# The last block of a hybrid encoder: pools divided by when their rows are done, operand buffers opened earlier, raw weights on another queue

## The chip, the cores and the metric

The kernel runs on one core of a Trainium2 chip. The metric is the device time of one execution in microseconds; of several runs the median is taken. The engines are PE (TensorE, matmuls; PEld is its weight load), DVE (VectorE), ACT (ScalarE), POOL (GpSimd) and SP (SyncE). Each has its own instruction stream and executes it in order. Here SP and POOL also issue the DMAs, each in the order of its own stream; "SPq" and "POOLq" in the profile are these DMA-issuing rows.

## The reference

One layer (DEPTH is 1) over 2048 prompt frames, 16 meta frames and 64 sample frames, all in f32, with D_MODEL = 1024 and D_FF = 2816:

```python
def _swiglu(h, wg, wu, wd):
    return (jax.nn.silu(h @ wg) * (h @ wu)) @ wd
...
        m, ns = _mixer(_rmsnorm(x, p['norm1_w'][l]), l, *st, segs, p)
        x = x + m
        x = x + _swiglu(_rmsnorm(x, p['norm2_w'][l]), p['w_gate'][l], p['w_up'][l], p['w_down'][l])
...
    return _rmsnorm(x, p['final_norm_w']), [jnp.stack(lst) for lst in new]
```

`_mixer` projects its input, runs three groups of recurrent heads (SSD, RWKV-7, HGRN2) and ends with the output projection `y @ w_out`. The change touches only that output projection and the SwiGLU of the last 1024 frames.

## The kernel before, in words

The prompt is cut into 17 tiles of 128 frames. Nine of them (EARLY, three blocks of three) get their output projection and their feed-forward part by the class of `fs`, beside the recurrent heads of later tiles; the last early block's feed-forward part (`fs[-1].ffn` from SWITCH on, then `fs[-1].rest()`) runs after all heads are done. The last eight tiles (LATE: two halves h of NH = 4 tiles) come then as one block, and everything below is about that block.

Every f32 product is made of three matmuls of values split in a high and a low part: ACT casts the high part (`S.activation`), DVE subtracts it for the low part. `to_parts` does that for operands, at L1416 (ACT) and L1417 (DVE), and `parts` for weights, at L1355 and L1356. All matmuls are issued by one helper, L111.

The block's matrices are taken in quarters: tokens by half, input columns by half, output columns by half. Instead of eight quarter products there are seven, listed in PRODS with operands a (a11, s3, s2, a22, s1, a12, s4: quarters of the left matrix or their sums and differences) and b (b11, t3, t2, t4, t1, b21, b22: quarters of the weights or their sums and differences t1 to t4). The b quarters were split before and lie in DRAM as pairs; SP loads them (L216, "w<-w", 512 KB). The t quarters are sums: those of "wo" and of the first PRE = 3 column pairs were prepared in DRAM, SP loads them (L1364) and `parts` splits them. For the later column pairs the four raw quarters are loaded (L1538, "lraw", 256 KB each), summed on DVE (L1540 to L1543) and split. All split weights go through a ring of WB = 5 buffers "w", raw ones through RB = 3 buffers "raw".

The steps of the block are:

1. "wo", by `tokens_first`: seven products into PSUM banks (g by `xbank`, d by `ybank`, four each), added on DVE to the rows `acc[h][j]`. Its operands are made by `y_group` from the mixers' outputs ya, in pairs, in tiles of `op_tile` ("op", four buffers in the pool lq). The sums s1, s2, s3, s4 of ya are made at L1458 to L1464.
2. `second_half` (beside the last products of "wo") and `first_half`: rows of the second and the first half are normalised (`scaled`, w2k at L246), transposed on PE (`turned`, L1480), and made into the operands `hop` of the columns; differences at L1511, L1512 and L1519.
3. `columns`, the gate and up projections by pairs of columns: class Pair steps a generator for gate and one for up side by side. Each of the seven steps is one product of 12 matmuls for gate and one for up. Results are copied out of PSUM by ACT (c11, c12, c21, c22 at L1558) or added on DVE (L1561); `finish` (L1610 to L1616) makes silu(gate) * up and its sums, and POOL stores them ("ma", "ms", L1619).
4. "wd", by `tokens_first` again, with operands loaded by SP in `m_group` (L1645); then the final norm. The t sums of w_down are made beside the columns: POOL loads the raw quarters (L1319, "raw<-in_w_down"), DVE sums them (L1327 to L1335), POOL stores them (L1324).

The order in each engine's stream is set by a scheduler that simulates the program; a tile of a pool that is opened on the place of an earlier one waits until the earlier one's users are done. Such pools are what the change moves: before, lq opens after `stE.close()` (the early block's pools), and lp (which holds c and lraw) opens on the place of the pool lo, whose rows first_half still uses.

Of the kernel before, what the change touches and what calls it, by code (L numbers as in the profile page):

```python
# [19 lines left out]
P = 128  # L20
# [58 lines left out]
def body(tc, A, O, blocks=None, supers=None, dbg=None):  # L79
# [7 lines left out]
    def pool(st, name, bufs=1, **kw):  # L87
        return st.enter_context(tc.tile_pool(name=name, bufs=bufs, **kw))
# [1195 lines left out]
    if supers:  # L1284
# [86 lines left out]
        def tokens_first(key, order, per, group, acc, then, ahead, behind):  # L1371
# [3 lines left out]
            for a, b, x, fresh, (h, d) in PRODS:  # L1375
# [32 lines left out]
                        behind(j)  # L1408
                then(a)

        def op_tile(tag="op"):
            o = mk(lq, [P, 2, 4, 512], F32, tag=tag, bufs=4) if tag == "op" else mk(lqa, [P, 2, 4, 512], F32, tag=tag, bufs=3)
            return o[:, 0].bitcast(F32R), o[:, 1].bitcast(F32R)

        def to_parts(hi, lo, src):
# [14 lines left out]
        for m in (2, 0, 1):  # L1430
            ya[m] = mk(lqa, [P, 2, 4, 512], F32, tag="ya", bufs=3)
            for h in range(2):
                for j in range(NH):
                    nc.sync.dma_start(ya[m][:, h, :, j * P:j * P + P], yscr[m][tile_of(h, j)])
        flow(fs[-1].ffn(SWITCH, NFF))
        flow(fs[-1].rest())
        stE.close()
        lq = pool(st, "lq", side="right", reuse_waits="tile")


        stO = ExitStack()
        lo_ = pool(stO, "lo", reuse_waits="tile")
        acc = [[mk(lo_, [P, D], tag=f"acc{h}{j}", bufs=1) for j in range(NH)] for h in (1, 0)][::-1]
        for h in (0, 1):
            for j in range(NH):
                G.dma_start(acc[h][j], x_rows(tile_of(h, j))[0][0])
# [58 lines left out]
        def first_half(j):  # L1505
# [10 lines left out]
            if j + 2 < NH:  # L1516
# [4 lines left out]

        tokens_first("wo", [4, 5, 0, 1, 2, 3], 2, y_group, acc, second_rows, second_half,
                     lambda j: scaled(0, j) if j < 2 else None)
        for n, tag in (("a11", "ya"), ("s3", "ya"), ("s2", "op"), ("a12", "op"), ("s4", "op")):
            hop[n] = op_tile(tag)


        msc = {(n, g): dram.tile([P, 4, 512], F32, tag=f"m{n}{g}", name=f"m{n}{g}") for n, *_ in PRODS for g in range(3)}
        stF = ExitStack()

        def columns(key, i):

            q = dict(zip(("b11", "b12", "b21", "b22"), quarters(key, i)))
            raw = {}
            if i >= PRE:
                for n in ("b22", "b12", "b11", "b21"):
                    raw[n] = mk(lp, [P, 512], tag="lraw", bufs=8)
                    nc.sync.dma_start(raw[n], q[n])  # L1538
                b11, b12, b21, b22 = (raw[n] for n in q)
                V.tensor_tensor(b22, b22, b12, SUB)  # L1540
                V.tensor_tensor(b12, b12, b11, SUB)
                V.tensor_tensor(b11, b22, b11, ADD)
                V.tensor_tensor(b21, b21, b11, SUB)  # L1543
                raw = {"t3": b22, "t1": b12, "t2": b11, "t4": b21}

            def prod(ps, a, b, first=True):
                hi, lo = parts(raw[b]) if b in raw else b_part(key, i, b)
                ah, al = hop[a]
                for k in range(4):
                    wh, wl = (x[:, k * P:(k + 1) * P] for x in (hi, lo))  # L1550
                    mm(ps, wh, ah[:, k], first and k == 0, False, not first)
                    mm(ps, wh, al[:, k], False, False, not first)
                    mm(ps, wl, ah[:, k], False, k == 3, not first)

            def copy(tag, ps, bufs):
                r = mk(lp, [P, 512], tag=tag, bufs=bufs)
                with tc.high_priority() if i < PRE else ExitStack():
                    S.activation(r, ps, AF.Copy)  # L1558
                return r

            add = lambda r, ps: V.tensor_tensor(r, ps, r, ADD)  # L1561
            pre = i < PRE
            x = xbank()
            prod(x, "s1", "t1")
            c22 = copy("c22", x, 6)
            yield
            y = xbank() if pre else ybank()
            prod(y, "a22", "t4")
            c21 = copy("c21", y, 6)
            yield  # L1570
            z = ybank()
            prod(z, "a11", "b11")
            c11 = copy("c11", z, 4)
            yield
            y = ybank()
            prod(y, "a12", "b21")
            add(c11, y)
            yield
            prod(z, "s2", "t2", False)
            c12 = copy("c12", z, 4)  # L1580
            yield
            if pre:
                add(c12, c22)
                x = xbank()
            prod(x, "s4", "b22", pre)
            add(c12, x)
            yield
            prod(z, "s3", "t3", False)
            add(c21, z)
            add(c22, z)  # L1590
            return c11, c12, c21, c22
# [28 lines left out]

        for j in range(NH):
            first_half(j)
        stO.close()
        lm = pool(st, "lm", side="right", reuse_waits="tile")
        lp = pool(stF, "lp", reuse_waits="tile")
        pairs = [Pair(i) for i in range(PRE)]
        for p_ in pairs:
            p_.step()
            p_.step()
        for i in range(NFF // 2):  # L1630
            if i >= PRE:
                pairs.append(Pair(i))
# [147 lines left out]
```

## Time and profile before

| what | value |
|---|---|
| median of 3 runs | 3547.19 us (3545.42 to 3551.86) |
| the profiled execution | 3539.1 us |
| its span | 3537.3 us |
| mean granted clock of PE | 0.982 |
| PE busy | 3367.3 us (95%) |
| POOL busy | 745.9 us (21%) |
| DMA moved | 860 MB, 243 GB/s over the span |

A row of a timeline has the start, the duration, the engine, the line of the kernel, the operation, the tiles out<-in, how many in a row, and in brackets the idle time before it and who ended it. A row of waits has the engine and the tile that waited, the one waited for, the total in us, how often, and the longest. A row of windows has, for each engine, busy time and count of instructions, and at the end the granted clock, the DMA share and GB/s. The last block runs from about 2726 us to the end.

### The profile page before, as it was taken

To read this page: it belongs to the slowest core of one execution; us is meant where nothing else is said; L and a number is where in the kernel's file an instruction comes from. 1 tells how busy PE (TensorE), PEld (TensorE's weight loads), DVE (VectorE), ACT (ScalarE), POOL (GpSimd) and SP (SyncE) were. 2 spreads that over 40 slices of the span, in tenths; PEclk is the share of its full clock that TensorE was granted. 3 is DMA by queue.
4 is the path that set the end of the run, shared out by engine and by line. 5 is a ranking of instruction groups with operands and counts; after the bars stand their busy time and mean duration, and the time that the engine had idled before them with its cause. 6 is when DMAs were issued, how large, how long until landed. Compare 5 with 4: busy or idle time off the path is not lost.

```text
span 3537.3 us, 61018 instructions
## 1 busy us (share of the span) xinstructions
PE 3367.3 (95%) x22588; PEld 2940.6 (83%) x22588; DVE 2216.0 (63%) x4961; ACT 1227.5 (35%) x2635; POOL 745.9 (21%) x1058
## 2 busy tenths in 40 slices
PE   7999999999999998889898999999989989999999
PEld 7999789899799996778786899879988868778887
DVE  3358556568666677687876767666524666555553
ACT  4445333244333444344342222222111352223342
POOL 3324202102112112444442120110101003320101
PEclk9999999999999998999999999999999999999999
DMA  9776875565775668888889898686688548775866
GB/s 323 232 229 212 296 228 166 162 174 171 247 225 172 193 198 266 290 308 302 298 312 329 308 325 269 208 286 220 222 278 261 185 141 284 272 264 170 289 202 214
DMA packets 431218, 860.41 MB, mean 243 GB/s; under 512 B 112432, under 2 KB 212280, under 8 KB 428872
## 3 DMA queue, kind: packets, MB, share of 16 engines
q1 hardware_dynamic: 403592, 765.79, 66.1%
q0 software_dynamic: 27328, 90.72, 6.9%
q8 instruction: 178, 2.92, 0.3%
q14 instruction: 120, 0.98, 0.1%
HBM read 603.81 MB, written 252.54 MB: 242 GB/s over the span
## 4 chain that ended last, share of the span: by engine, by line
PE 64%; DMA 13%; DVE 11%; issue 6%; POOL 2%; ACT 2%; SPq 2%; POOLq 0%; DVEq 0%; ACTq 0%
PE g L111 46%; PE d L111 8%; PE c L111 4%; PE h L111 3%; DMA w<-w 3%; DMA raw<-in_w_down 2%; DVE tp L640 1%; DVE Xp L641 1%; DMA hin<-hg 1%; DMA raw<-in_w_up 1%; POOL w L222 1%; DMA hg<-stage 1%; DVE gcv L418 1%; DMA dec<-cu 1%; DVE acc L1278 0%
## 5 line engine op out<-in xcount | busy, mean ns | idle before, releaser
L111 PE MATMUL g<-hhi,w 128*128 128x384 f32 (+3 forms) x3312 | 832.0, 330 | 10.3 <-DMA w<-w 4.1
L111 PEld LDWEIGHTS g<-hhi,w 128*128 128x128 f32 (+1 forms) x3312 | 579.9, 188 | 24.3 <-POOL w L222 4.3
L111 PE MATMUL g<-h2hi,w 128*128 128x384 f32 (+1 forms) x2112 | 549.5, 336 | 19.5 <-DMA w<-w 6.7
L111 PE MATMUL g<-hlo,w 128*128 128x384 f32 (+3 forms) x1680 | 551.2, 328 | 0.0
L111 PEld LDWEIGHTS g<-h2hi,w 128*128 128x128 f32 x2112 | 376.6, 190 | 33.4 <-ACT w L220 7.7
L111 PE MATMUL g<-h2lo,w 128*128 128x384 f32 (+1 forms) x1056 | 349.9, 332 | 0.0
L111 PEld LDWEIGHTS g<-hlo,w 128*128 128x128 f32 (+1 forms) x1680 | 313.9, 187 | 6.8 <-issue 0.9
L222 POOL TENSOR_TENSOR w<-raw,w 128x512 fp32r<-128x512 f32 x180 | 246.7, 1373 | 343.8 <-ACT w L220 273.0
L111 PE MATMUL g<-w,mhi 128*128 128x512 f32 x792 | 259.2, 403 | 12.0 <-DMA w<-w 4.0
L220 ACT ACTIVATE w<-raw 128x512 fp32r<-128x512 f32 x240 | 150.3, 629 | 207.9 <-PE g L111 58.3
L111 PEld LDWEIGHTS g<-h2lo,w 128*128 128x128 f32 x1056 | 200.4, 190 | 2.9
L111 PE MATMUL g<-w,op 128*128 128x512 f32 x816 | 194.4, 397 | 3.1 <-ACT op L1416 3.1
L111 PEld LDWEIGHTS g<-w,op 128*128 128x128 f32 x816 | 153.4, 189 | 41.6 <-ACT op L1416 3.5
L111 PEld LDWEIGHTS g<-w,mhi 128*128 128x128 f32 x792 | 144.5, 188 | 48.3 <-DVE acc L1278 7.6
L111 PE MATMUL g<-w,hhi 128*128 128x512 f32 (+1 forms) x544 | 176.3, 404 | 7.4 <-DMA w<-w 4.3
L111 PE MATMUL d<-op,w 128*128 128x512 f32 x720 | 168.8, 392 | 2.8 <-DVE w L1356 2.8
L111 PEld LDWEIGHTS d<-op,w 128*128 128x128 f32 x720 | 135.0, 188 | 33.5 <-DVE w L1356 4.1
L1278 DVE TENSOR_TENSOR acc<-g,acc 128x512 f32<-128x512 f32 (+1 forms) x198 | 132.1, 682 | 44.0 <-PE g L111 43.9
L640 DVE TENSOR_TENSOR tp<-Xp,b4k 128x60 f32<-128x60 f32 (+24 forms) x527 | 126.8, 241 | 51.2 <-DMA b4k<-psc 38.3
L111 PE MATMUL g<-w,mlo 128*128 128x512 f32 x396 | 155.6, 393 | 0.0
L111 PE MATMUL d<-w,op 128*128 128x512 f32 x612 | 143.9, 395 | 0.0
L111 PEld LDWEIGHTS d<-w,op 128*128 128x128 f32 x612 | 114.7, 187 | 28.1
(437 smaller groups left out, 6233.0 us busy)
## 6 DMA issues: line engine op xcount, KB each, us to landing
w<-w SPq DMA_DIRECT2D x893, 512.0 KB, 4.4
hin<-hg SPq DMA_DIRECT2D x16, 1280.0 KB, 8.4
rin<-rw SPq DMA_DIRECT2D x16, 896.0 KB, 7.1
raw<-in_w_gate SPq DMA_DIRECT2D x56, 256.0 KB, 4.5
raw<-in_w_up SPq DMA_DIRECT2D x56, 256.0 KB, 4.5
hg<-stage SPq DMA_DIRECT2D x64, 192.0 KB, 2.5
raw<-in_w_out SPq DMA_DIRECT2D x48, 256.0 KB, 4.6
sin<-ss SPq DMA_DIRECT2D x16, 768.0 KB, 4.9
```

Of the source, the lines that this page charges most:

```text
L111: return T.matmul(out, lhsT, rhs, start=start, stop=stop, skip_group_check=more)
L220: S.activation(hi, raw, AF.Copy)
L222: (G if units[0] % 4 < GLO else V).tensor_tensor(lo, raw, wt[:, 0], SUB)
L418: V.scalar_tensor_tensor(cvt[:, :M], raw[:, j:j + M], tap(j), cvt[:, :M], MUL, ADD)
L640: V.tensor_tensor(tv, _bc(Xp[:, 0:m, q], 2, w), _bc(Up[:, q, q + 1:32], 1, m), MUL)
L641: V.tensor_tensor(Xp[:, 0:m, q + 1:32], Xp[:, 0:m, q + 1:32], tv, ADD)
L1278: V.tensor_tensor(self.acc[:n, i, cs], ps[:n], self.acc[:n, i, cs], ADD)
```

## The change

There are three parts.

- Operand tiles: three buffers "op" in lq, which is opened before the early block's last part (`fs[-1].ffn`); every fourth operand tile instead lies in "opx", one buffer in a pool lqx, opened where lq was.
- Pools by when their rows are done: the second half's rows acc[1] lie in a pool of their own (lo1), closed right after "wo". On that place a new pool lc holds c21 and c22 (c22 with four buffers instead of six). The pool of the other rows is closed, and lm and lp are opened, only after the early steps of the first three pairs. For these pairs the first step is now a22·t4 (c21) and the second s1·t1 (c22), and the last of them does only its first step ahead, so that ten products instead of twelve stand before the first a11·b11.
- lraw: ten buffers instead of eight, loaded from POOL's stream instead of SP's (64 loads).

```diff
         def op_tile(tag="op"):
-            o = mk(lq, [P, 2, 4, 512], F32, tag=tag, bufs=4) if tag == "op" else mk(lqa, [P, 2, 4, 512], F32, tag=tag, bufs=3)
+            if tag == "op":
+                opn[0] += 1
+                p, tag, bufs = (lq, "op", 3) if opn[0] % 4 else (lqx, "opx", 1)
+            else:
+                p, bufs = lqa, 3
+            o = mk(p, [P, 2, 4, 512], F32, tag=tag, bufs=bufs)
...
+        lq = pool(st, "lq", side="right", reuse_waits="tile")
         flow(fs[-1].ffn(SWITCH, NFF))
         flow(fs[-1].rest())
         stE.close()
-        lq = pool(st, "lq", side="right", reuse_waits="tile")
-        stO = ExitStack()
+        lqx = pool(st, "lqx", side="right", reuse_waits="tile")
+        stO, stO1, stF = ExitStack(), ExitStack(), ExitStack()
         lo_ = pool(stO, "lo", reuse_waits="tile")
-        acc = [[mk(lo_, [P, D], tag=f"acc{h}{j}", bufs=1) for j in range(NH)] for h in (1, 0)][::-1]
+        lo1 = pool(stO1, "lo1", side="right", reuse_waits="tile")
+        acc = [[mk((lo_, lo1)[h], [P, D], tag=f"acc{h}{j}", bufs=1) for j in range(NH)] for h in range(2)]
...
         tokens_first("wo", [4, 5, 0, 1, 2, 3], 2, y_group, acc, second_rows, second_half,
                      lambda j: scaled(0, j) if j < 2 else None)
+        stO1.close()
+        lc = pool(stF, "lc", side="right", reuse_waits="tile")
...
                 for n in ("b22", "b12", "b11", "b21"):
-                    raw[n] = mk(lp, [P, 512], tag="lraw", bufs=8)
-                    nc.sync.dma_start(raw[n], q[n])
+                    raw[n] = mk(lp, [P, 512], tag="lraw", bufs=10)
+                    G.dma_start(raw[n], q[n])
...
-                r = mk(lp, [P, 512], tag=tag, bufs=bufs)
+                r = mk(lc if tag[1] == "2" else lp, [P, 512], tag=tag, bufs=bufs)
...
-            x = xbank()
-            prod(x, "s1", "t1")
-            c22 = copy("c22", x, 6)
-            yield
-            y = xbank() if pre else ybank()
-            prod(y, "a22", "t4")
-            c21 = copy("c21", y, 6)
-            yield
+            def second(first):
+                nonlocal x, c21, c22
+                if first:
+                    y = xbank() if pre else ybank()
+                    prod(y, "a22", "t4")
+                    c21 = copy("c21", y, 6)
+                else:
+                    x = xbank()
+                    prod(x, "s1", "t1")
+                    c22 = copy("c22", x, 4)
+            x = c21 = c22 = None
+            for first in (pre, not pre):
+                second(first)
+                yield
...
         for j in range(NH):
             first_half(j)
-        stO.close()
-        lm = pool(st, "lm", side="right", reuse_waits="tile")
-        lp = pool(stF, "lp", reuse_waits="tile")
         pairs = [Pair(i) for i in range(PRE)]
         for p_ in pairs:
             p_.step()
-            p_.step()
+            if p_ is not pairs[-1]:
+                p_.step()
+        stO.close()
+        lm = pool(st, "lm", reuse_waits="tile")
+        lp = pool(stF, "lp", reuse_waits="tile")
```

The lines of the changed kernel stand 7 to 19 lower than those of the kernel before (L1416 becomes L1423, L1538 becomes L1548, L1558 becomes L1568, L1619 becomes L1637).

How the streams change, at three places. The first is ACT's stream in the early block's last part, where w2k and mhi belong to that block (its activation at L1240 and the cast of the result at L1243). Before:

```order
L1240 ACTIVATE w2k_28292<-g_28226 128x384
L1243 ACTIVATE mhi_28148<-w2k_28292 128x384
L1240 ACTIVATE w2k_28414<-g_28356 128x384
L1243 ACTIVATE mhi_28354<-w2k_28414 128x384
L1240 ACTIVATE w2k_28478<-g_28420 128x384
L1243 ACTIVATE mhi_28354<-w2k_28478 128x384
```

And after the change:

```order
L1240 ACTIVATE w2k_28292<-g_28226 128x384
L1243 ACTIVATE mhi_28148<-w2k_28292 128x384
L1423 ACTIVATE op_29272<-ya_28736 128x1024
L1240 ACTIVATE w2k_28414<-g_28356 128x384
L1243 ACTIVATE mhi_28354<-w2k_28414 128x384
L1423 ACTIVATE op_29303<-ya_28745 128x1024
L1240 ACTIVATE w2k_28478<-g_28420 128x384
L1243 ACTIVATE mhi_28354<-w2k_28478 128x384
L1423 ACTIVATE op_29334<-ya_28754 128x1024
```

Three casts of operands of "wo", which stood behind the early block's last rows, now stand between its activations.

The second is ACT's stream at the end of first_half (casts into ya and op from hraw or from the transposed rows d), with the copies c of the early products. Before:

```order
L1416 ACTIVATE ya_30190<-hraw_4220_29260 128x4x128
L1416 ACTIVATE op_30193<-hraw_4220_29260 128x4x128
L1416 ACTIVATE op_30191<-hraw_4221_29261 128x4x128
L1416 ACTIVATE op_30193<-hraw_4220_29260 128x4x128
L1558 ACTIVATE c_4391_30358<-g_30340 128x512
L1558 ACTIVATE c_4399_30398<-g_30380 128x512
L1558 ACTIVATE c_4395_30378<-g_30360 128x512
L1558 ACTIVATE c_4403_30418<-g_30400 128x512
```

And after the change:

```order
L1568 ACTIVATE c_4411_30461<-g_30443 128x512
L1423 ACTIVATE op_30203<-hraw_4220_29266 128x4x128
L1423 ACTIVATE op_30201<-hraw_4221_29267 128x4x128
L1568 ACTIVATE c_4415_30481<-g_30463 128x512
L1423 ACTIVATE ya_30199<-d_30320 128x4x128
L1423 ACTIVATE opx_30202<-d_30333 128x4x128
L1423 ACTIVATE op_30203<-hraw_4220_29266 128x4x128
L1568 ACTIVATE c_4419_30501<-g_30483 128x512
L1423 ACTIVATE ya_30200<-hraw_4220_29266 128x4x128
L1423 ACTIVATE op_30201<-hraw_4221_29267 128x4x128
L1568 ACTIVATE c_4423_30521<-g_30503 128x512
L1423 ACTIVATE op_30203<-hraw_4220_29266 128x4x128
```

The copies, all of which stood behind first_half's last cast, now stand among its casts.

The third is SP's stream in the computed pairs, with the loads of split weights w and of raw quarters lraw. Before:

```order
L216 DMA w_31720<-w_17882 128x1024
L216 DMA w_31735<-w_17975 128x1024
L1538 DMA lraw_31857<-in_w_up 128x512
L1538 DMA lraw_31859<-in_w_up 128x512
L1538 DMA lraw_32122<-in_w_gate 128x512
L1538 DMA lraw_32124<-in_w_gate 128x512
L1538 DMA lraw_32126<-in_w_gate 128x512
L1538 DMA lraw_32128<-in_w_gate 128x512
L216 DMA w_31920<-w_18207 128x1024
L216 DMA w_31937<-w_18297 128x1024
```

In the changed kernel SP has the loads of w there:

```order
L216 DMA w_31947<-w_18297 128x1024
L216 DMA w_31964<-w_18228 128x1024
L216 DMA w_31980<-w_18316 128x1024
L216 DMA w_32029<-w_18361 128x1024
L216 DMA w_32044<-w_18453 128x1024
L1664 DMA mraw_33724<-ma_30205 128x1024
```

and POOL's stream has the raw quarters, between the stores of the pairs (ma, ms) and the loads and stores of the w_down sums (raw, wd):

```order
L1637 DMA ms_30207<-c_4545_31363 128x512
L1637 DMA ms_30210<-c_4553_31429 128x512
L1637 DMA ms_30216<-c_4536_31311 128x512
L1324 DMA wd5t_32117<-raw_32112 128x512
L1637 DMA ms_30222<-c_4539_31329 128x512
L1324 DMA wd5t_32122<-raw_32114 128x512
L1324 DMA wd5t_32125<-raw_32119 128x512
L1548 DMA lraw_31867<-in_w_up 128x512
L1319 DMA raw_32127<-in_w_down 128x512
L1548 DMA lraw_31869<-in_w_up 128x512
L1319 DMA raw_32411<-in_w_down 128x512
L1324 DMA wd5t_32130<-raw_32127 128x512
```

The raw loads have left SP's stream and stand in POOL's, where they are issued in turn with those stores and loads.

More of the change, by code (lines that the diff above doesn't have):

```diff
@@ L1409, in tokens_first @@
                 then(a)
+        opn = [0]
         def op_tile(tag="op"):
-            o = mk(lq, [P, 2, 4, 512], F32, tag=tag, bufs=4) if tag == "op" else mk(lqa, [P, 2, 4, 512], F32, tag=tag, bufs=3)
+            if tag == "op":
[4 more added lines that the diff above has]
+            o = mk(p, [P, 2, 4, 512], F32, tag=tag, bufs=bufs)
             return o[:, 0].bitcast(F32R), o[:, 1].bitcast(F32R)
@@ L1528, in body @@
         msc = {(n, g): dram.tile([P, 4, 512], F32, tag=f"m{n}{g}", name=f"m{n}{g}") for n, *_ in PRODS for g in range(3)}
-        stF = ExitStack()
         def columns(key, i):
```

## The prediction, made before the changed kernel was run

> **What bounds the kernel now.** I read the page first, then the waits of PE (TensorE) in the last block (from 2590 us on), then the timelines of the engines at the places that these waits name, and last the waits of the engine that was late there. The page's first row:
>
> ```profile
> PE 3367.3 (95%) x22588; PEld 2940.6 (83%) x22588; DVE 2216.0 (63%) x4961; ACT 1227.5 (35%) x2635; POOL 745.9 (21%) x1058
> ```
>
> PE is the bound, so time can come only from PE's idle 5%, or from what makes its matmuls slow. The waits of PE from 2590 us to the end, each with its total, its count and its longest:
>
> ```profile
> PE g L111 <- ACT c L1558: 10.0, 1, 10.0
> PE g L111 <- DMA w<-w: 8.2, 6, 3.2
> PE d L111 <- DMA w<-w: 5.0, 3, 2.0
> PE d L111 <- DVE w L1356: 4.9, 4, 2.1
> PE g L111 <- ACT op L1416: 3.1, 1, 3.1
> PE g L111 <- ACT ya L1416: 3.0, 1, 3.0
> ```
>
> They fall into three places that the diff touches: the start of the output projection (A, the op row), the turn from it to the columns (B, the c row), and the first computed pairs (C, most of the DMA and DVE rows). Most of the 8.2 lies near 2600 us, where nothing is changed.
>
> **A: operand buffers beside the early block.** PE, ACT and SP around the start of "wo", the landing time of the weights there, and the window behind the idle time (PE, PEld, DVE, ACT, POOL, then granted clock, DMA share, GB/s):
>
> ```profile
> 2729.46 18.83 PE L111 MATMUL g<-w,op 128*128 128x512 f32 x72 [3.11 <-ACT op L1416]
> 2728.37 2.94 ACT L1416 ACTIVATE op<-ya 128x1024 fp32r<-128x1024 f32 x3
> 2724.32 0.32 SPq L216 DMA_DIRECT2D w<-w  x1
> w<-w SPq DMA_DIRECT2D x14, 512.0 KB, 4.1
> 2730.00:2735.00 5.00, 4.97 (x15) 3.45 (x14) 5.00 (x7) 1.38 (x3) 3.86 (x8) 0.66 1.02 392
> ```
>
> ACT casts the first operands at 2728.37, when the early block has ended, because their pool opens only then; PE stands 3.11 us. Then the granted clock is 0.66 for a while: 72 matmuls take 18.83 us. The pace at full clock, from place B's rows below, is (2907.42 - 2890.94) / 72 = 0.229 us, so 16.5 was due and 2.4 us went to the slow clock. On the table: 3.1 + 2.4 = 5.5 us. With three buffers opened before the early block's rest, three casts (1.0 us each) and their low parts on DVE run up to 100 us earlier. Late next is the second weight load: issued at 2724.32, with 4.1 us to landing it is there at 2728.4; PE, which would end the early block at 2726.4 (2729.46 - 3.11), spends 9 x 0.229 = 2.1 us on the first weight and gets to it at 2728.4. So 0 to 1 us of wait stays. What the moved casts could cost: they stand in ACT's row between the early block's tanh rows and need the loads of ya:
>
> ```profile
> L1434 SPq DMA_DIRECT2D ya<-y x24: 518/634/1887, 2601.8 to 2630.3; - x24
> DMA to landing us min/median/max: 5.2/7.4/8.7
> 2630.91 0.52 ACT L1243 ACTIVATE mhi<-w2k 128x384 fp32r<-128x384 f32 x1 [9.50 <-DVE w2k L1242]
> ```
>
> The last third lands near 2639 (2630.3 + 8.7), and an L1243 behind a cast would be late by at most some 2 us beside idle stretches of 9.5 us on ACT. The fourth, eighth ... tile (opx, one buffer) may hold an operand back later, near the w_down steps where PE has no idle now; 0 to 3 us, taken as 0, since operands there are made some groups ahead. A = 5.5 - 0.5 - 1 = **4 us** (ends: 1 and 5.5).
>
> **B: products beside first_half.** PE, then ACT and DVE, then a window:
>
> ```profile
> 2856.50 1.22 PE L111 MATMUL g<-ya,w 128*128 128x512 f32 x2 [3.03 <-ACT ya L1416]
> 2871.82 0.63 PE L1480 MATMUL d<-ident,w2k 128*128 128x128 f32 x4 [0.69 <-DVE w2k L246]
> 2873.08 0.63 PE L1480 MATMUL d<-ident,w2k 128*128 128x128 f32 x4 [0.63 <-DVE w2k L246]
> 2883.74 7.36 PE L111 MATMUL g<-ya,w 128*128 128x512 f32 x24 [10.03 <-ACT c L1558]
> 2890.94 5.66 PE L111 MATMUL g<-op,w 128*128 128x512 f32 x24
> 2907.42 5.66 PE L111 MATMUL d<-ya,w 128*128 128x512 f32 x24
> 2883.11 2.04 ACT L1558 ACTIVATE c<-g 128x512 f32<-128x512 f32 x4
> 2882.46 1.47 DVE L1417 TENSOR_TENSOR op<-hraw,op 128x512 fp32r<-128x512 f32 x2
> 2860.00:2880.00 20.00, 12.38 (x65) 9.78 (x63) 18.95 (x33) 11.36 (x23) 1.38 (x2) 0.92 0.23 67
> ```
>
> A product is 12 matmuls, 2.745 us; each row of 24 is two. Four products of the first pairs run before 2871, one for each g bank; the banks empty only at 2883.11, when the ACT copies have a place, since the pool of c opens where first_half's rows were. Until then DVE works through first_half without a gap (18.95 of 20) and PE stands 0.69 + 0.63 + 10.03 = 11.35 us; the 24 matmuls behind take 7.20 (2890.94 - 2883.74) instead of 5.49, 1.7 more. On the table: 13.1 us.
>
> With c21 and c22 in their own pool (on rows that are done after "wo") the copies go at once, and 10 of the 12 early products stand before the first a11. Six of them after the first four are 16.5 us, more than the 11.35 of the hole: PE is filled to 2883.74 + 16.5 - 11.35 = 2888.9, and then needs a11. DVE ends first_half at 2883.93 now; it gets six more low parts there (0.7 each by the 2882.46 row, 4.2 us): 2888.1. So the cover is just enough; if DVE is a few us later, it shows as a wait before a11. ACT has 8.6 us free of 20 for six copies and six casts of the same size (0.5 each, 6 us). The swap of a22·t4 and s1·t1 costs no matmul. The 3.03 us at 2856.50 stand as they are. B = 13.1 - 1.1 for DVE's row = **12 us**. Ends: 6, if each copy, now between first_half's rows on ACT, holds these back by a part of its product; 16, if the 3.03 goes too.
>
> **C: raw weights through POOL.** SP, PE, windows with and without idle, DVE's waits in the first of these, then POOL's largest wait, its raw loads and the landing times there:
>
> ```profile
> 3066.99 13.08 SPq L1538 DMA_DIRECT2D lraw<-in_w_gate  x4
> 3080.16 1.91 SPq L216 DMA_DIRECT2D w<-w  x4
> 3084.34 7.37 PE L111 MATMUL d<-ya,w 128*128 128x512 f32 x24 [1.99 <-DMA w<-w]
> 3020.00:3180.00 160.00, 148.73 (x633) 118.92 (x632) 93.76 (x150) 41.03 (x74) 42.74 (x79) 0.99 0.78 269
> 3180.00:3340.00 160.00, 160.00 (x699) 130.76 (x698) 85.12 (x125) 52.88 (x83) 19.90 (x37) 1.00 0.65 223
> DVE raw L1327 <- DMA raw<-in_w_down: 17.1, 3, 7.1
> DVE raw L1335 <- DMA raw<-in_w_down: 9.4, 4, 4.5
> DVE lraw L1541 <- DMA lraw<-in_w_up: 9.2, 4, 4.6
> DVE raw L1335 <- DMA ms<-c: 7.6, 1, 7.6
> DVE raw L1330 <- DMA raw<-in_w_down: 5.4, 3, 2.0
> DVE lraw L1543 <- DMA lraw<-in_w_up: 4.4, 2, 3.3
> DVE lraw L1540 <- DMA lraw<-in_w_gate: 3.8, 2, 2.4
> POOL ma L1619 <- DVE c L1610: 19.9, 8, 8.9
> L1319 POOL DMA_DIRECT2D raw<-in_w_down x25 | 13.6, 543 | 27.6 <-DMA wd7t<-raw 7.8 <-DMA wd9t<-raw 6.3 <-DMA wd8t<-raw 4.5
> raw<-in_w_down POOLq DMA_DIRECT2D x25, 256.0 KB, 5.3
> lraw<-in_w_gate SPq DMA_DIRECT2D x16, 256.0 KB, 4.7
> ```
>
> SP issues in order. Four lraw loads, whose buffers are not free yet, hold it for 13 us, the weight loads behind them leave at 3080.16, and PE waits for one at 3084.34. From 3020 to 3180 PE idles 160 - 148.73 = 11.27 us, and the slow clock behind the 1.99 takes about 1.7 more (7.37 where 5.66 is the rule): 13 us on the table. Behind 3180, where the w_down sums on POOL and DVE are done, PE has none, with the same lraw loads on SP.
>
> This tells of a second cause beside SP. DVE's seven rows add up to 56.9 us, 39.5 on the raw of w_down and 17.4 on lraw; with 93.76 busy its row fills 150.7 of 160 us, so DVE has hardly run ahead and each late load reaches PE. The change takes w off the blocked queue, and two more buffers let the next pair's loads go sooner, so most of the 17.4 should go; the work of 147 us (160 - 13) then meets 93.8 + 39.5 = 133 on DVE, 14 us of room. Against that, POOL issues 64 loads more at 0.543 us, 35 us over some 400, and does it in order between raw loads, stores that wait on DVE (19.9 in eight waits) and round trips. A lraw load behind such a wait is late by up to 8.9 us, less than four products (11 us), the lead that the five weight buffers give; but raw loads behind a lraw load without a free buffer are late too, and the 39.5 can grow. I keep about two thirds: C = **9 us**. Ends: 0 and 13 (a loss is the last rival).
>
> The Trainium skill, "DMA: Bandwidth & Descriptors", section "Issuing engines are not separate DMA queues", says that DMAs started by several engines run on the same 16 DMA engines, and that this saves only the sequencer's time to start them. By that rule C would bring nothing and the time would be the first rival's; the SP rows speak against it, since there the queue is held not by the starting but by a wait in its row.
>
> On the clock, the Trainium skill, "TensorE: Matmul & The Clock Gate", section "What's actually happening", lets the clock fall after an idle window of about 3.4 us. By it A would give 3.1 in place of 5.5 before deductions and C 11.3 in place of 13, together 4 us less; the row at 3084.34, slow behind 1.99 us, disagrees.
>
> **Sum.** 4 + 12 + 9 = 25 us. The profiled execution took 3539.1 us (span 3537.3), 8.1 below the median of the runs, 3547.2; I take the difference over: 3514.1 profiled, 3522 as median.
>
> **Rivals.**
> 1. C stays as it is: DVE remains the pace setter, because POOL's loads come as late as SP's did. For it: 150.7 of 160, and the largest waits are on loads that POOL issues already. Against it: the 3066.99 row. 4 + 12 = 16 us: 3531.
> 2. First_half becomes the bound in B: ACT's copies, in its row, wait for products and hold DVE back. For it: 18.95 of 20 on DVE. Against it: ACT's idle time. 4 + 6 + 9 = 19: 3528.
> 3. The change does little: A's wait turns into one for w, B gives its lower end and C nothing, 1 + 6 = 7: 3540.
> 4. Slower: POOL's single row delays the w_down sums. DVE has 160 - 150.7 = 9 us to spare; with lraw waits as now and 39.5 doubled, PE loses 39.5 - 9.3 = 30 us in C, against A + B of 16: 14 more, 3561. It turns the sign from about 16 + 9 = 25 us more on DVE, one us for each of the 25 raw loads; for it are POOL's waits in order, against it that POOL is busy only 42.74 of 160.
>
> **How the numbers follow.** Forecast 0.57, rival 1 0.20, rival 2 0.08, rival 3 0.07, rival 4 0.08. A measurement of this kernel can tell about 0.2%, 7 us. Faster by more than that: the first three cases, 0.85; within it: rival 3, 0.07; slower: 0.08. Low end: all upper ends, 5.5 + 16 + 13 = 34.5, 3512.7, less the 1.8 by which the lowest run lies under the median: 3511. High end: the lower ends with 1 us from C, 8 us: 3539. That holds the forecast and the first two rivals, 0.85, less the tail.
>
> **What would show it.** A: no idle of 3 us at the start of "wo", a granted clock near 1 there. B: products without a gap over 40 us, c copies among first_half's rows, and at most 2 us before the first a11. C: no row of SP's waits on lraw, PE's waits on w and L1356 under 4 us from 3000 to 3160, DVE's lraw waits small. Wrong would be: DVE's waits for raw over 60 us there, a new PE wait for ACT in the early block, SP held at mraw by POOL's stores, or an idle before a11 over 5 us.

## The result, and the profile after

Over six runs each, the kernel takes 3520.36 us as median (3511.97 to 3527.06) against 3552.2 before; the ratio is 0.9913, with a 95% interval of 0.9895 to 0.9932. That is 31 us less (0.0087 x 3552), with 24 to 37 us in the interval. The profiled execution has a span of 3510.2 us against 3537.3. The page's first row after:

```profile
PE 3366.0 (96%) x22588; PEld 2942.8 (84%) x22588; DVE 2212.6 (63%) x4961; ACT 1226.9 (35%) x2635; POOL 778.5 (22%) x1122
```

PE's busy time over the whole span is the same to about 1 us, but the head of the kernel, where nothing is changed, hides a part: from the last transposition L880 to the end PE is busy for 884.8 us instead of 893.1 and idle for 24.9 instead of 46.9. Idle time is what went in the main; of the other 8 us about 7 are slow clock (1.9 in A, twice 1.7 in B, 1.7 in C). PE's waits from 2660 us to the end, all there are:

```profile
PE g L111 <- ACT w L1355: 2.1, 2, 1.3
PE g L111 <- DMA w<-w: 0.9, 1, 0.9
PE g L111 <- ACT op L1423: 0.8, 1, 0.8
PE g L111 <- DVE op L1424: 0.3, 1, 0.3
```

The head of the kernel, where nothing is changed, differs between executions by some us, so the stages are compared between landmarks on PE: the last transposition of the heads' input (L880), the second group of "wo", the first product a11, the first product of w_down, and the end. The rows of the kernel before that the prediction did not show, then those after:

```profile
2597.24 0.60 PE L880 MATMUL h<-ident,hin 128*128 128x128 f32 x4
2748.12 16.96 PE L111 MATMUL d<-w,op 128*128 128x512 f32 x72
3312.92 28.16 PE L111 MATMUL g<-w,op 128*128 128x512 f32 x120
```

```profile
2600.50 0.60 PE L880 MATMUL h<-ident,hin 128*128 128x128 f32 x4
2746.07 5.76 PE L111 MATMUL d<-w,opx 128*128 128x512 f32 x24
2883.11 5.66 PE L111 MATMUL d<-ya,w 128*128 128x512 f32 x24
3282.25 22.56 PE L111 MATMUL g<-w,op 128*128 128x512 f32 x96
```

Stage A is L880 to the second group of "wo": 2748.12 - 2597.24 = 150.9 before, 145.6 after. B goes from there to the first a11, C to the first product of w_down, D to the end. Where twelve instead of ten early products stand before a11, two products (5.5 us) are counted in C. A stage in which nothing was changed can differ by up to 1.9 us between two executions (A in e3), so less than 2 us in A, C or D is not read as an effect; B is steadier (137.0 to 137.1 in the nine kernels with divided pools and the new order). The table has all kernels of this study, each from its one profiled execution, with the ratio to the kernel before where runs were timed:

| kernel | A | B | C | D | ratio and interval |
|---|---|---|---|---|---|
| before | 150.9 | 153.8 | 411.0 | 224.4 | |
| changed | 145.6 | 137.0 | 399.1 | 228.0 | 0.9913 (0.9895 to 0.9932) |
| e1 operands alone | 145.6 | 154.0 | 417.0 | 225.7 | 0.9994 (0.9983 to 1.0006) |
| e2 pools alone | 150.9 | 137.1 | 415.6 | 224.5 | 0.9964 (0.9945 to 0.9982) |
| e3 POOL's queue alone, 8 buffers | 152.8 | 154.3 | 395.5 | 226.8 | 0.9971 (0.9956 to 0.9987) |
| e4 operands and pools | 145.7 | 137.1 | 413.5 | 225.4 | 0.9944 (0.9925 to 0.9964) |
| e5 changed, raw loads on SP, 10 buffers | 147.0 | 137.0 | 407.5 | 225.2 | 0.9944 (0.9919 to 0.9969) |
| e6 changed, 8 buffers | 145.6 | 137.0 | 401.6 | 227.1 | 0.9926 (0.9897 to 0.9955) |
| e7 changed, more work on DVE | 146.2 | 137.1 | 412.1 | 228.0 | |
| e8 changed, w_down sums later | 145.5 | 137.1 | 399.0 | 227.2 | 0.9900 (0.9874 to 0.9926) |
| e9 changed, old order of early products | 146.1 | 140.8 | 400.5 | 227.4 | |
| e10 changed, w_up's raw loads on SP | 145.9 | 137.0 | 405.6 | 224.4 | 0.9916 (0.9888 to 0.9943) |
| e11 changed, later pairs' raw loads on SP | 146.0 | 137.0 | 403.5 | 224.8 | 0.9929 (0.9899 to 0.9959) |

After against before: A -5.3, B -16.8, C -11.9, D +3.6, together -30.4, which is the measured 31.

**A.** The casts in the early block on ACT, and "wo" on PE:

```profile
2613.14 1.06 ACT L1423 ACTIVATE op<-ya 128x1024 fp32r<-128x1024 f32 x1 [12.02 <-DMA ya<-y]
2636.09 1.06 ACT L1423 ACTIVATE op<-ya 128x1024 fp32r<-128x1024 f32 x1 [1.42 <-DMA ya<-y]
2729.27 16.96 PE L111 MATMUL g<-w,op 128*128 128x512 f32 x72
```

The last of the three casts is done 92 us before PE needs it. No idle stands ahead of the 72 matmuls, and they take 16.96 us (18.83 before), so the slow clock is gone with the wait: 3.1 and 1.9 us of the 5.3.

**B.** PE at the first early product and ahead of a11, the first and the ninth of the ten early copies on ACT, the end of first_half on DVE, and the window of the turn:

```profile
2852.22 0.74 PE L111 MATMUL g<-op,w 128*128 128x512 f32 x2 [0.80 <-ACT op L1423]
2877.62 5.66 PE L111 MATMUL g<-op,w 128*128 128x512 f32 x24
2856.14 0.60 ACT L1568 ACTIVATE c<-g 128x512 f32<-128x512 f32 x1 [0.21 <-PE g L111]
2880.56 0.60 ACT L1568 ACTIVATE c<-g 128x512 f32<-128x512 f32 x1 [0.19 <-PE g L111]
2880.95 1.48 DVE L1424 TENSOR_TENSOR op<-hraw,op 128x512 fp32r<-128x512 f32 x2
2860.00:2880.00 20.00, 20.00 (x97) 16.54 (x96) 19.47 (x34) 13.91 (x28) 0.86 (x1) 1.00 0.44 137
```

Copies leave 2.5 to 4.5 us apart from 2856 on, no product waits for a bank, and PE is busy for 20.00 of 20 us where it was 12.38. DVE is as full as before (19.47), and yet first_half ends at 2882.43, just before the tenth product does (2883.11).

**C.** The columns beside the w_down sums (the window shows the same order of busy times as before), SP's row, DVE's largest waits in that window, the waits at the raw loads (SP's in the window 3020 to 3180 of the kernel before, then POOL's here), and their landing times:

```profile
2980.00:3140.00 160.00, 160.00 (x701) 131.28 (x700) 102.08 (x162) 47.28 (x83) 67.04 (x125) 1.00 0.85 296
3013.27 47.01 SPq L216 DMA_DIRECT2D w<-w  x10
DVE raw L1330 <- DMA raw<-in_w_down: 15.7, 8, 3.8
DVE lraw L1551 <- DMA lraw<-in_w_up: 15.1, 4, 4.5
DVE raw L1335 <- DMA raw<-in_w_down: 13.3, 7, 2.7
SPq L1538 <- DVE w L1356: 118.9, 27, 12.0
POOL lraw L1548 <- DVE w L1356: 14.6, 9, 2.5
lraw<-in_w_gate POOLq DMA_DIRECT2D x16, 256.0 KB, 4.0
lraw<-in_w_up POOLq DMA_DIRECT2D x16, 256.0 KB, 5.3
```

PE has no idle in 160 us where it had 11.27. SP's row is nothing but w for 47 us. In that window POOL waits 14.6 us at raw loads, 2.5 at the longest, where SP waited 118.9, 12.0 at the longest. From 2880 to 3320 us POOL waits 90.5 us at them, 14.0 at the longest, but no load of w stands behind these.

**What is left, and what is worse.** Two waits near the last early product, and the rows of SP that lead to them; then DVE's last instruction before and after, and POOL's closing instructions (DRAIN) before, in e10 (32 more loads on POOL) and after (64 more). A DRAIN row has the count, the shortest, median and longest in ns, and the first and last start in us:

```profile
2939.53 3.30 PE L111 MATMUL g<-ya,w 128*128 128x512 f32 x12 [1.31 <-ACT w L1355]
2943.61 3.42 PE L111 MATMUL g<-ya,w 128*128 128x512 f32 x12 [0.78 <-ACT w L1355]
2929.44 0.32 SPq L1664 DMA_DIRECT2D mraw<-ma  x1
2934.88 0.32 SPq L1364 DMA_DIRECT2D raw<-w_gate2t  x1
```

```profile
3532.60 1.41 DVE L1142 SCALAR_TENSOR_TENSOR acc<-acc,rs,nw 128x512 f32<-128x512 f32 x2 [0.73 <-POOL rs L230]
```

```profile
3503.07 1.41 DVE L1142 SCALAR_TENSOR_TENSOR acc<-acc,rs,nw 128x512 f32<-128x512 f32 x2 [0.73 <-POOL rs L230]
```

```profile
L1776 POOLq DRAIN  x3: 40/93/1734, 3532.0 to 3537.1; - x3
L1795 POOLq DRAIN  x3: 40/102/4344, 3516.1 to 3521.2; - x3
L1795 POOLq DRAIN  x3: 40/102/6957, 3502.5 to 3509.9; - x3
```

The clock at the two waits is at full speed (1.00 from 2939.53 to 2947.04). From DVE's last row to the end it is 4.7 us before and 7.1 after: 2.4 us of the 3.6 that D lost. The longest DRAIN is the first of POOL's three. It takes 1.73 us before, 4.34 in e10 and 6.96 after, 2.61 more for each 32 loads. In all three kernels the end comes 0.8 us behind the later of two: this DRAIN (3533.7, 3520.4 and 3509.4) and SP's own first DRAIN, behind the last stores (3536.5, 3520.6 and 3507.0). Only after the change is POOL's the later one, by 2.4 us. What a DRAIN waits for isn't shown. Most of the rest of D is a wait of 0.90 us for w near the first operand in opx; e6, e8, e10 and e11 have the same operand tiles and no such wait, so opx isn't shown to be its cause.

### The profile page after: what moved, and what is told of

It reads as the page before. It is cut to its first block, busy times and chain, and to the rows that moved or that the text cites. A ratio compares the mean times of both kernels' runs of the same rounds, so it can differ in the third digit from the quotient of the medians.

```text
span 3510.2 us, 61013 instructions
## 1 busy us (share of the span) xinstructions
PE 3366.0 (96%) x22588; PEld 2942.8 (84%) x22588; DVE 2212.6 (63%) x4961; ACT 1226.9 (35%) x2635; POOL 778.5 (22%) x1122
## 4 chain that ended last, share of the span: by engine, by line
PE 69%; DMA 11%; DVE 10%; issue 4%; ACT 2%; POOL 2%; SPq 2%; POOLq 0%; DVEq 0%; ACTq 0%
PE g L111 47%; PE d L111 11%; PE c L111 5%; PE h L111 4%; DMA w<-w 3%; DMA raw<-in_w_up 1%; DMA hin<-hg 1%; POOL w L222 1%; DMA hg<-stage 1%; DVE tp L640 1%; DVE Xp L641 1%; DMA raw<-in_w_gate 1%; PE po L111 1%; DVE acc L1278 1%; DVE gcv L418 1%
## 5 line engine op out<-in xcount | busy, mean ns | idle before, releaser
L111 PE MATMUL g<-w,op 128*128 128x512 f32 x600 | 142.8, 395 | 0.0
L111 PEld LDWEIGHTS g<-w,op 128*128 128x128 f32 x600 | 112.3, 187 | 27.3
L641 DVE TENSOR_TENSOR Xp<-Xp,tp 128x60 f32<-128x60 f32 (+24 forms) x527 | 122.9, 233 | 13.3
L230 POOL TENSOR_TENSOR rs<-ss,half 128x1 f32<-128x1 f32 (+2 forms) x51 | 34.6, 681 | 424.6 <-DVE ss L228 261.0
L111 PEld LDWEIGHTS g<-w,hhi 128*128 128x128 f32 (+1 forms) x544 | 99.5, 189 | 32.4 <-DMA w<-w 6.5
L356 DVE SCALAR_TENSOR_TENSOR stage<-graw,cvec,stage 128x384 f32<-128x384 f32 (+2 forms) x98 | 53.5, 549 | 113.5 <-ACT graw L351 34.4
```

What stands on the lines that cost most here:

```text
L111: return T.matmul(out, lhsT, rhs, start=start, stop=stop, skip_group_check=more)
L230: G.tensor_tensor(rs[:n], ss[:n], half[:n, 0:w], ALU.pow)
L356: V.scalar_tensor_tensor(st[:, a0:a1], raw[:, s0:s0 + a1 - a0], mu, st[:, a0:a1], MUL, ADD)
L641: V.tensor_tensor(Xp[:, 0:m, q + 1:32], Xp[:, 0:m, q + 1:32], tv, ADD)
```

## The experiments

**e1 to e4: the parts apart.** e1 has only the new op_tile with lq opened earlier and lqx; e2 only the pools lo1 and lc with the new order of the early products; e4 both. e3 is the kernel before with one line changed:

```diff
-                    nc.sync.dma_start(raw[n], q[n])
+                    G.dma_start(raw[n], q[n])
```

> Only the operand part: lq with three op buffers opened before the early block's rest, every fourth operand in lqx. Theory (the three parts act at three places and add up): the start of wo has no idle time and no slow clock, as in the changed kernel, where the first 72 matmuls took 16.96 us in place of 18.83; 5 us are gained (3.1 + 2.4 at most 5.5), ratio about 0.9985, and the two other places stay: about 11 us idle before the copies of c, about 11 us idle in the first computed pairs. Rival (the start only moves the wait: first_half is bound by DVE, so what is won at the start is given back at the turn): idle at the turn grows by 3 to 5 us and the time stays within 1 us.

> Only the pools divided by when their rows are done, with the new order of the early products; operands and raw loads as before. Theory: the turn gains 14 to 17 us (13.1 of idle and slow clock by the profile before, plus 2 of the 3.0 us before the first early product, which only the order a22 t4 first can have saved), ratio about 0.9955; the start of wo keeps its 3.1 us of idle and the first computed pairs their 11. Rival (the two extra operands made early, or the raw loads moved off SP, gave part of the turn's gain): the turn gains 8 us or less.

> Only the queue: raw quarters issued by POOL, with the eight buffers of before (ten have no room without the divided pools). Theory (SP's row, blocked by raw loads without a free buffer, is the cause in the first computed pairs): PE's idle from 3020 to 3180 us falls from 11.3 to under 4 us, 8 to 12 us are gained with the slow clock, ratio about 0.997. Rival (the two extra buffers are what matters, or DVE's full row): the idle stays over 8 us, now with PE waiting for DVE instead of for w, and the time stays within 3 us.

> The operand part and the pools, raw loads still issued by SP with eight buffers. Theory (parts add): 5 + 16 = 21 us gained, ratio 0.994; the first computed pairs keep 9 to 13 us of idle, which start earlier by those 21 us. Rival (the gain at the turn feeds the columns faster and the stall there grows, since what PE wins at the turn it loses to the blocked row): idle in the first computed pairs over 16 us and a gain under 16 us.

A is -5.3 us wherever the operands are made early (e1, e4), B is -16.8 wherever the pools are divided (e2, e4), each to 0.3 us, and neither moves the other; the rivals that part of B came from elsewhere or that A comes back in B fall. In C, with the raw loads on SP, the profiled executions of e1, e2 and e4 lost 6.0, 4.6 and 2.5 us to the kernel before. Operands alone are worth nothing that can be measured (0.9994), though the interval still holds the 0.9985 that was expected; e4 came out at the ratio expected of parts that add up (0.9944 for 0.994), and its rival (over 16 us of idle, a gain under 16) did not occur: PE is idle for 12.0 us in all of C. PE in C of e1:

```profile
3094.11 7.36 PE L111 MATMUL d<-ya,w 128*128 128x512 f32 x24 [1.97 <-DMA w<-w]
3154.21 7.38 PE L111 MATMUL g<-op,w 128*128 128x512 f32 x24 [1.78 <-DMA w<-w]
3182.24 7.67 PE L111 MATMUL d<-ya,w 128*128 128x512 f32 x24 [0.67 <-DMA w<-w]
```

The waits are about as long as before (12.3 us in sum over ten rows; 11.27 before), but three groups run at the slow clock behind them instead of one: four stretches of 3.41 us at half speed fall in C, where it was one, and each costs 1.7 us. So about 5 of e1's 6.0 us are the clock. Where such a stretch falls differs from execution to execution (last section), so this loss can't be laid to the operands. e3 shows the other side: C in 395.5 us, which is 144 products at 2.746, so nothing is lost at all. Its window over that stage:

```profile
2912.00:3302.00 390.00, 390.00 (x1706) 320.01 (x1705) 229.28 (x358) 122.31 (x205) 116.72 (x216) 1.00 0.75 252
```

The queue alone, without the two buffers, thus takes back all 15.5 us that C lost before. Of the whole kernel it is about 10 us (0.9971), as A and D of that execution are longer by 1.9 and 2.4. That it is the order on SP and not quicker transfers shows in the landing of w over the stage, before and in e3:

```profile
w<-w SPq DMA_DIRECT2D x68, 512.0 KB, 6.2
w<-w SPq DMA_DIRECT2D x68, 512.0 KB, 5.6
```

A load of w lands 0.6 us sooner, little against waits of up to 12.0. What changed is what SP waits for at w: in C, for PE to free a buffer, 86.7 us before and 215.0 in e3. SP now waits for the ring of w to turn and not at a raw load.

**e5, e6 and e10: queue or buffers.** e5 and e6 are the changed kernel with one half of the third part undone, e10 splits the loads:

```diff
# e5
-                    G.dma_start(raw[n], q[n])
+                    nc.sync.dma_start(raw[n], q[n])
# e6
-                    raw[n] = mk(lp, [P, 512], tag="lraw", bufs=10)
+                    raw[n] = mk(lp, [P, 512], tag="lraw", bufs=8)
# e10
-                    G.dma_start(raw[n], q[n])
+                    (G if key == "w_gate" else nc.sync).dma_start(raw[n], q[n])
```

> The changed kernel, with ten raw buffers, but SP issues the raw quarters again. Theory (SP's blocked row is the cause): PE keeps 8 to 14 us of idle in the first computed pairs, in part waiting for w, as with eight buffers; SP waits over 60 us at its raw loads there; from the first a11 to the first w_down product it takes 404 to 409 us (399 in the changed kernel). Rival (two more buffers let the loads go soon enough from either queue): under 4 us of idle after the early products, about 399 us for that stretch.

> The changed kernel with eight raw buffers instead of ten, issued by POOL. Theory (the queue is what matters, the buffers not): no idle in the computed pairs beyond the two waits of 2.1 us near the last early product, the stretch from the first a11 to the first w_down product within 2 us of the changed kernel's 399, ratio to before as the changed kernel's (0.991). Rival (in the whole change the buffers carry the gain, since POOL's row has more to wait for): 4 us or more of new idle, PE waiting for DVE.

> The changed kernel with the raw quarters of w_gate issued by POOL and those of w_up by SP. Theory (each load without a free buffer in SP's row holds w behind it): idle in the computed pairs between those of POOL alone (2.1 us) and of SP alone (7 us), the stretch from the first a11 to the first w_down product 401 to 406 us. Rival (it is enough that one of two groups leaves SP): 399 us or less. The time from the last DVE instruction's start to the end, 4.7 us where SP issues all of them and 7.1 us where POOL does: about 5.9 if it grows with POOL's number of loads, 7.1 or 4.7 if it goes by a step.

Ten buffers on SP (e5) give 407.5 us in C: two more buffers are worth 6.0 of e4's 413.5, but 12 us over e3's full pace stay. SP's waits at the raw loads in e5, from 2880 to 3320 us, and in e10, from 2900 to 3300:

```profile
SPq L1548 <- DVE w L1356: 181.7, 51, 12.0
```

```profile
SPq L1548 <- DVE w L1356: 154.6, 28, 17.4
```

In e5 the idle after the early products is 3.9 us, less than the 8 to 14 expected of all of C, with 3.5 more near the last early product; the theory was right in the stretch and too high in idle (by the idle alone, the rival's "under 4 us" came true). Half of the loads on SP (e10) hold the row for 154.6 us, and C is 405.6, as expected between the two. Eight buffers on POOL (e6) give 401.6, 2.5 more than ten (2 were expected at most), of which most lies in the waits near the last early product. C follows SP's waits at the raw loads through the kernels that have parts A and B: 203.6 us of waits and 413.5 in C (e4), 181.7 and 407.5 (e5), 154.6 and 405.6 (e10), 97.9 and 403.5 (e11), none and 399.1 (changed). So the queue is the cause. The two buffers are worth 6.0 us while SP has the loads, and on POOL's queue 2.5 us, not far above what executions differ by (e9, changed only at the turn, has 400.5).

**e7: is DVE a second pace setter?** Behind each w_down sum stand 14 subtractions on a scratch tile, whose result nothing uses.

```diff
+        idle = mk(lp, [P, 256], tag="idle", bufs=1)
+        V.memset(idle, 0.0)
...
             t_sums(f"wd{i}", quarters("wd", i), G)
+            for _ in range(14):
+                V.tensor_tensor(idle, idle, idle, SUB)
```

> The changed kernel with 14 more subtractions of 128x256 on DVE behind each of the 11 w_down sums (a scratch tile; the result of the kernel does not use them), about 0.35 us each, 5 us for a pair, 20 us in 160. Theory that the prediction held (DVE's row, work plus waits, is a second pace setter: 155 of 160 us are filled in the changed kernel): PE loses 10 us or more over the first computed pairs. Rival (DVE's waits stretch only because it has time; its row gives way): under 3 us lost.

C grows from 399.1 to 412.1, by 13 us for 51 us of DVE work (285.1 us busy against 234.1). PE waits for it:

```profile
3038.42 2.58 PE L111 MATMUL d<-op,w 128*128 128x512 f32 x10 [2.65 <-DVE w L1356]
3119.73 2.58 PE L111 MATMUL d<-op,w 128*128 128x512 f32 x10 [1.36 <-DVE w L1356]
```

Another 4.10 us of idle stand at the last early product, where it was 2.1 in the changed kernel. DVE's row is close behind PE's pace, as the prediction held, but three quarters of the added work found room.

**e8: the waits near the last early product.**

```diff
-            t_sums(f"wd{i}", quarters("wd", i), G)
+            if i >= 2:
+                t_sums(f"wd{i - 2}", quarters("wd", i - 2), G)
+        for i in range(NFF // 2 - 2, NFF // 2):
+            t_sums(f"wd{i}", quarters("wd", i), G)
```

> The changed kernel with each w_down sum two pairs later in the program (the sum for pair i is written behind pair i + 2, the last two behind the last pair). Theory (the 2.1 us of idle near the last early product come from the prepared sums of w_gate and w_up that share three raw buffers with the w_down sums): those waits go, with the slow clock behind them 3 to 4 us; the stretch from the first a11 to the first w_down product falls from 399 to about 395.5 us. Rival (SP's row is held there by a load that waits for one of POOL's stores): they stay, within 1 us. A risk of both: the last sums come late for w_down and PE waits there.

The two waits go, as the theory had it. That alone doesn't settle the cause, since in e8 the first loads of w_gate2t and w_up2t also stand ahead of SP's load of mraw. SP's rows in the changed kernel speak against the rival: the load of mraw (L1664) waited 10.0 us for POOL's store and left at 2929.44, but the load of w_gate2t behind it left only at 2934.88, after 5.0 us more of waiting for the store of a w_down sum, which holds one of the shared buffers. The stretch does not shorten (399.0 for 395.5): the clock was at full speed at these two waits, so the slow clock that the theory wanted to win back wasn't there, and three other waits, 2.5 us in sum, stand later in C, the first of them for DVE. The ratio, 0.9900, can't be told from the changed kernel's.

**e9: the order of the early products.**

```diff
-                    c21 = copy("c21", y, 6)
+                    c21 = copy("c21", y, 4)
...
-                    c22 = copy("c22", x, 4)
+                    c22 = copy("c22", x, 6)
...
-            for first in (pre, not pre):
+            for first in (False, True):
```

> The changed kernel with the old order of the early products, s1 t1 before a22 t4 (six buffers for c22 and four for c21, since now all three pairs make c22 ahead). Theory (a22 is ready sooner than s1, so the new order lets PE start the first early product sooner): the idle before the first early product returns from 0.8 to about 3 us, and the stretch from the second group of wo to the first a11 grows by about 2 us from 137.0; the rest of the turn stays without idle. Rival (the first operand is not what ended that wait): idle of 0.8 us as in the changed kernel, 137 us.

The idle is back (3.52 us), and B is 140.8 instead of 137.0:

```profile
2872.24 0.74 PE L111 MATMUL g<-ya,w 128*128 128x512 f32 x2 [3.52 <-ACT ya L1423]
```

So the swap is worth 3.7 us of B's 16.8, 1.7 more than expected, since the clock is slow again behind the wait (0.70 from 2872.24 to 2876.00).

**e11: the late end.**

```diff
-                    G.dma_start(raw[n], q[n])
+                    (G if i < 7 else nc.sync).dma_start(raw[n], q[n])
```

> The changed kernel with POOL issuing the raw quarters only of the pairs 3 to 6, which stand beside the w_down sums, and SP those of pairs 7 to 10 (32 loads each). Theory (SP's row hurts only where DVE is held by the w_down sums; the late end goes by a step in the number of POOL's loads): no new idle, the stretch from the first a11 to the first w_down product stays within 1.5 us of 399, and from the last DVE start to the end 4.7 us instead of 7.1, so 2.4 us less than the changed kernel. Rival (SP's row hurts in every pair): 3 us or more of idle in the later pairs, waiting for w, and no gain.

The end comes 4.7 us after DVE's last row, as with SP and as in e10 (both have 32 loads on POOL; with 64 it is 7.1 to 7.2 in all six kernels). It looks like a step, but POOL's first DRAIN grows evenly, and with 32 loads it still ends before SP's own end. But C is 403.5, 4.4 longer: 2.7 us of idle come back from 3107 us on, first this one:

```profile
3107.64 3.00 PE L111 MATMUL d<-ya,w 128*128 128x512 f32 x12 [1.11 <-DMA w<-w]
```

The first theory is wrong in that SP's row hurts there too (it waits 97.9 us for its 32 loads), and this version is no gain over the changed kernel (0.9929).

## Why the prediction was right, and where its terms were off

- The time (3522 for 3520.4), the sign and the range held, and the three places gained by the mechanisms that the prediction named. That the time is right to 1.6 us is in part luck: the sum was 25 us and about 31 came, but the median of the kernel before, from which the forecast started, is 3552.2 over six runs instead of 3547.2. The terms miss in both directions.
- A: forecast 4, measured 5.3. The 5.5 on the table took the pace of the columns (0.229 us a matmul) for "wo", whose rows of 72 take 16.96 us at full clock too, so the slow clock cost 1.9 and not 2.4. Both deductions, 0.5 for w and 1 for ACT's row, were not needed: the first group of "wo" starts without a wait, and the casts moved into the early block, though they waited for ya (12.02 us at the first), held nobody: the early block ends 2.9 us later than before (2729.27 against 2729.46 - 3.11), and L880, ahead of them, was already 3.3 later.
- B: forecast 12, measured 16.8, above the upper end of 16. The mis-sized step is "The 3.03 us at 2856.50 stand as they are" with "the swap ... costs no matmul": e9 shows that a22·t4 first is worth 3.7 us. The wait had a slow clock behind it (0.51 from 2856.50 to 2860.00 in the kernel before), which the prediction didn't count. The 13.1 of idle and slow clock went whole; the 1.1 taken off for DVE's row did not show.
- C: forecast 9, measured 11.9 against before, and 14.3 against e4, the kernel that the third part really met. That SP's blocked row is the cause is shown (e3, e5, e10). The step that failed is "most of the 17.4 should go": DVE still waits 17 us for lraw in 160 (15.1 at L1551 alone), and its row is filled as before. What fell is all its waits for the same work: 62.7 us per 148.7 of PE's work before (the prediction's 56.9 were the seven largest), 55.2 per 160 after. e7 bears out the second pace setter. Of the ends of 0 and 13 the upper was low: the whole loss was 15.5. The prediction's 11.3 of idle and 1.7 of slow clock are all that C has of them; the other 2.5 us lie in matmuls that run longer around the waits, without idle that the rows count.
- D was forecast at 0. It lost 3.6: 2.4 at the very end, by POOL's DRAIN, which no step held, and 0.9 in a wait for w near an operand in opx (bounded at 3 and taken as 0; its cause isn't shown).
- Of the rivals, the first (C stays) is refuted by C's window and by e3, the second (first_half becomes the bound) by the 20.00 of 20, the third (little changes) by A and B, and the fourth by DVE's waits for the raw quarters of w_down, which fell from 39.5 us to 29.6 (15.7 + 13.3 + 0.6) instead of growing. What spoke for the fourth was real in part: the raw loads of w_up take 5.3 us to land where SP's took 3.8 (those of w_gate 4.0 for 4.7), and DVE waits as long for them as before. One sign that the prediction had named as wrong appeared: at mraw SP waits 39.4 us for POOL's stores from 2880 to 3320 us (21.5 before). It did little harm: PE's only idle behind it is the 2.1 and 0.9 us above.
- The Trainium skill's sentence in "DMA: Bandwidth & Descriptors", section "Issuing engines are not separate DMA queues", that another engine saves only the time to start a transfer, would have C unchanged. e3 measures 15.5 us. Starting 64 loads costs 21 us of SP's row (0.33 us each); SP's waits at them were 204.6 us from 2880 to 3320 us. What the other queue saves is the wait in order ahead of w.
- On the clock, the Trainium skill, "TensorE: Matmul & The Clock Gate", section "What's actually happening", gives an idle window of about 3.4 us. The traces show less, and that the length alone doesn't decide: behind 1.97 us of idle 24 matmuls take 7.36 us in e1, and behind 1.99 us they take 5.77 in e4. The last section has the rule that they do show.

## What to carry to other kernels

Look for the queue that waits in order before you count its transfers: a load whose buffer is not free holds every load behind it, and moving such loads to another queue was worth 15.5 us of one stage with no buffer more (about 10 us of the whole). Copies out of PSUM need a place that is free when the product ends, not when the last user of a larger pool ends; dividing a pool by when its rows are done filled a hole of 13 us. Judge a part by its own stage as well as by the whole time: in e1 the operands gave 5.3 us in theirs, and slow stretches of the clock in another took them back in that execution.

## What the runs showed of the hardware that was not expected

**POOL's end.** The first DRAIN of POOL's closing instructions grew by 2.61 us for each 32 DMAs that moved to POOL (1.73, 4.34 and 6.96 us), in all thirteen kernels alike, although POOL had issued its last DMA more than 50 us before. It costs time only once it outlasts SP's own end, here by 2.4 us with 64 loads. What it does in that time stays open.

**The clock.** Between 2640 and 3420 us of these traces the granted clock drops to half for 3.41 us or a multiple of it, and the drops of one execution lie on one grid of that step: in e1 they start at 3094.20, 3155.64 and 3179.53, which is 18 and 7 steps. What counts is PE's idle time within one step of the grid, not the length of one wait. Two steps in e1 (a wait of 1.97 us lies in the first), then two in e4 (a wait of 1.99 us is cut, 0.67 us before the first and 1.32 in it; the grid there is counted back 12 steps from e4's drop at 3119.37):

```profile
3090.79:3094.20 3.41, 1.45 (x7) 0.85 (x6) 3.41 (x6) 1.11 (x2) 0.74 (x2) 1.00 1.00 362
3094.20:3097.61 3.41, 3.41 (x8) 2.70 (x9) 3.22 (x6) 0.00 (x0) 1.96 (x4) 0.50 0.99 311
```

```profile
3078.41:3081.82 3.41, 2.09 (x9) 1.76 (x10) 3.38 (x7) 0.48 (x1) 1.93 (x4) 1.00 1.04 328
3081.82:3085.23 3.41, 3.41 (x17) 2.79 (x16) 1.23 (x3) 1.12 (x2) 0.29 (x2) 1.00 1.01 394
```

In that range of all thirteen traces, each of the 23 steps at full clock with 1.78 us of idle or more was followed by a slow one, and none of the others, which had 1.73 at most. The grid lies elsewhere in each execution, so a wait of about 2 us may cost 1.7 us more or nothing.
